# The first norm and the first projection of a decoder trunk: GpSimd taken out, statistics straight from the squares

## The chip, the cores and the metric

The kernel runs on one core of a Trainium2 chip. The metric is device time in microseconds (us), from one launch to its end. The core's engines are TensorE (PE, matrix products; PEld marks its weight loads), VectorE (DVE), ScalarE (ACT), GpSimd (POOL) and SyncE (SP, whose queue issues the transfers). They run side by side, and each works through its own queue in order.

## The reference

Two layers of a decoder trunk, on one sequence of 512 tokens with 1024 features, in float32. Each layer is three sublayers: a feed-forward block (SwiGLU, 2816 hidden), a token mixer, and a second feed-forward block. What the change touches is the start of the first one:

```python
def _rmsnorm(x, g):
    y = x * lax.rsqrt(jnp.mean(x * x, axis=-1, keepdims=True) + EPS)
    return y * g

mod = silu(c) @ ada_w[l] + ada_b[l]          # shift, scale, gate for each sublayer

def _sublayer(x, fn, pre_g, post_g, shift, scale, gate, res_w):
    h = _rmsnorm(x, pre_g) * (1.0 + scale) + shift
    y = _rmsnorm(fn(h), post_g)
    return x + res_w * (1.0 + gate) * y

def _swiglu(h, w13, w2):
    g, u = jnp.split(h @ w13, 2, axis=-1)
    return (silu(g) * u) @ w2
```

## The kernel before, in words

Features lie on the 128 partitions, tokens along the free dimension, so x is eight tiles `xs[f]` of 128x512. Precision comes from splitting both sides of a product: a weight tile is rounded to a high part `wh` (ScalarE, `L250`) and the remainder `wl` (a subtraction, `L251`), h likewise to `hh` and `hl`, and each product is three matmuls: `hh` by `wh`, `hh` by `wl`, `hl` by `wh`.

The first norm and the head of the first feed-forward phase stand in one block in which the program's order is kept on PE, DVE, ACT and SP:

- The conditioning vector c is spread over the partitions by two one-row products (`L1060`) and passed through SiLU into `cb` (`spread`, `L1055` and `L1056`). `spin(n)` issues n products into a bank that nobody reads; `WARM` gives the three counts.
- ACT squares each x tile (`L1079`). Seven additions on POOL and DVE (`add`, `L1072`) bring eight squares down to two tiles, and PE sums those over the partitions into a 128x4 tile `st` (`L1088`): four products of one column per tile, each recorded twice.
- `rsqrt` (`L274` to `L287`) takes the root in nine tiny DVE steps. `rms_bcast` (`L307`) brings it back to the feature layout as `bc`, in PSUM; ACT copies that to `bcs` (`L1112`).
- `ada_block(0, typ, f)` loads 512 KB of the conditioning weights (SP, `L144`) and multiplies them by `cb` with a sum along the row (DVE, `L145`). `ada_fin` turns the sum into one column of scale (two DVE steps, `L155` and `L156`) and one of shift (one step, `L153`).

Then the head: eight steps f. The weights `raw` of step f (512 KB, `L239`, fetched a step ahead) are split, ACT for `wh` and POOL for `wl`. `pre_h` makes h in three steps: DVE forms `tmp` = x times scale column times root (`L340`), ACT adds the shift and rounds to `hh` (`L341`), DVE takes the rest as `hl` (`L342`). The two conditioning products of step f + 1 stand on DVE around `L342`, then its `ada_fin`. PE then runs 24 matmuls of 512 columns into eight banks that stay open over all steps (`mm_start`, `L442`, for the first seven steps, and `mm_k`, `L264` to `L266`, for the last).

The conditioning blocks share two rings of eight buffers with the weights' high and low parts, and raw weights use a ring of four: a load is issued when the tile that had its buffer is done with. SP issues in program order, so a load that waits holds up those behind it. Behind the head, `evac` takes each pair of banks (`L477` to `L479`, `L256`, `L257`), and the remaining 18 pairs follow with PE alone in written order; conditioning loads for later phases are mixed into DVE's work there, using the same four raw buffers.

Of the kernel before, what the change touches and what calls it, by code (L numbers as in the profile page):

```python
# [7 lines left out]
F32 = mybir.dt.float32  # L8
F32R = mybir.dt.float32r
I32 = mybir.dt.int32  # L10
AF = mybir.ActivationFunctionType
ALU = mybir.AluOpType
ADD, SUB, MUL, MAX, MIN = ALU.add, ALU.subtract, ALU.mult, ALU.max, ALU.min

P = 128
D = 1024
T = 512
KT = D // P
# [22 lines left out]
LATE, LATE_Y = 3, 1  # L41
W_0, W_A, W_ST, W_BC, W_UP, W_SQ, W_H = 1.606, 0.51, 1.903, 0.459, 0.81, 2.2, 0.868

WARM = (3, 1, 3)
SPREAD = (1, 3)
NGRP = 7

# [28 lines left out]
def trunk_kernel(ctx: ExitStack, tc: tile.TileContext, a: dict, out: bass.AP):  # L76
    nc = tc.nc
    V, S, PE, G = nc.vector, nc.scalar, nc.tensor, nc.gpsimd

    cst = ctx.enter_context(tc.tile_pool(name="cst", bufs=1))  # L80
# [10 lines left out]
    def t_tmp(w=T):  # L91
        if w == 256:
            return sb.tile([P, w], F32, tag="tmph", bufs=TMPH, name=nm("tmph"))
        return sb.tile([P, w], F32, tag="tmp", bufs=TMP, name=nm("tmp"))
# [16 lines left out]
    def t_st():  # L111
        return ps.tile([P, T], F32, tag="st", bufs=2, name=nm("st"))
# [9 lines left out]
    def vc(name, i=0, w=None):  # L122
        o, n = _OFF[name]
        return vec[:, o + i : o + i + (n - i if w is None else w)]
# [12 lines left out]
    def dcol(ph, typ, f, w=1):  # L137
        o = ph * 24 + typ * 8 + f
        return drv[:, o : o + w]

    def ada_block(ph, typ, f, w=None):
        i = ph * 24 + typ * 8 + f
        w = t_raw() if w is None else w
        nc.sync.dma_start(w, a["ada_w"][i])  # L144
        V.scalar_tensor_tensor(w, w, 0.5, cb, op0=MUL, op1=MUL, accum_out=modc[:, i : i + 1])  # L145

    def ada_fin(ph, typ, f, w):
        i = ph * 24 + typ * 8 + f
        m = modc[:, i : i + w]
        d = dcol(ph, typ, f, w)  # L150
        n = ph * 8 + f
        if typ == 0:
            V.tensor_tensor(d, m, vc("ada_b", i, w), op=ADD)  # L153
            return
        V.tensor_tensor(m, m, vc("ada_b", i, w), op=ADD)  # L155
        V.scalar_tensor_tensor(d, m, 1.0, vc("pre" if typ == 1 else "post", n, w), op0=ADD, op1=MUL)  # L156
        if typ == 2 and ph % 3 != 1:
            V.tensor_scalar(d, d, 0.5, None, op0=MUL)
# [83 lines left out]
    def t_w():  # L242
        return (
            sb.tile([P, 1024], F32R, tag="wh", bufs=8, name=nm("wh")),
            sb.tile([P, 1024], F32R, tag="wl", bufs=8, name=nm("wl")),
        )
# [23 lines left out]
    def rsqrt(src, scale):  # L270

        w = src.shape[1]
        v, y, q, t = t_small(w), t_small(w), t_small(w), t_small(w)
        V.tensor_scalar(v, src, scale * RS_LAM, EPS * RS_LAM, op0=MUL, op1=ADD)  # L274
        V.tensor_scalar(y.bitcast(I32), v.bitcast(I32), -0.5, RS_K, op0=MUL, op1=ADD)
        V.tensor_tensor(q, y, y, op=MUL)
        if w <= 2:
            for i in range(w):
                c = slice(i, i + 1)
                V.tensor_scalar(q[:, c], q[:, c], v[:, c], -RS_M, op0=MUL, op1=ADD)  # L280
        else:
            V.tensor_tensor(q, q, v, op=MUL)
            V.tensor_scalar(q, q, -RS_M, None, op0=ADD)
        V.scalar_tensor_tensor(t, q, RS_B[0], q, op0=ADD, op1=MUL)
        V.scalar_tensor_tensor(t, t, RS_B[1], q, op0=ADD, op1=MUL)
        V.scalar_tensor_tensor(t, t, RS_B[2], q, op0=ADD, op1=MUL)
        V.scalar_tensor_tensor(y, t, RS_B[3], y, op0=ADD, op1=MUL)  # L287
        return y
# [14 lines left out]
    def rms_bcast(y):  # L303
        n = y.shape[1]
        bc = t_st()
        for i in range(n):
            PE.matmul(  # L307
                bc[:, i * P : (i + 1) * P], lhsT=y[:, i : i + 1].to_broadcast([P, P]), rhs=ident, start=True, stop=True
            )
        return bc[:, : n * P]  # L310
# [3 lines left out]
    class SumSq:  # L314
# [7 lines left out]
        def add(self, src):  # L322
            self.n += 1
            if self.n == 1:
                t = t_tmp(T) if self.w == T else sb.tile([P, 256], F32, tag="acc", bufs=3, name=nm("acc"))
                self.acc = t
            else:
                t = t_tmp(self.w)
            S.activation(t, src, AF.Square)  # L329
            if self.n > KT - self.late:  # L330
                self.queue.append((t, lambda: V.tensor_tensor(self.acc, self.acc, t, op=ADD)))
            elif self.n > 1:
                G.tensor_tensor(self.acc, self.acc, t, op=ADD)  # L333
# [5 lines left out]
    def pre_h(ph, f, bc, lo, hi, t):  # L339
        V.scalar_tensor_tensor(t, xs[f][:, lo:hi], dcol(ph, 1, f), bc, op0=MUL, op1=MUL)  # L340
        S.activation(hh[f][:, lo:hi], t, AF.Identity, bias=dcol(ph, 0, f))  # L341
        return lambda: V.scalar_tensor_tensor(  # L342
            hl[f][:, lo:hi], t, dcol(ph, 0, f), hh[f][:, lo:hi].bitcast(F32), op0=ADD, op1=SUB
        )
# [69 lines left out]
    class PairHead(Ready):  # L414
# [21 lines left out]
        def mm_start(self, k):  # L436

            ops = [(b, (2 * p + s) * P) for p in range(self.n) for s, b in enumerate(self.banks[0][p])]
            order = [(0, hh[k]), (0, hl[k]), (1, hh[k])] if k == 0 else [(0, hh[k]), (1, hh[k]), (0, hl[k])]
            for i, (part, h) in enumerate(order):  # L440
                for b, c in ops:
                    PE.matmul(  # L442
                        b, lhsT=self.w[k][part][:, c : c + P], rhs=h, start=(k == 0 and i == 0),
                        stop=(k == KT - 1 and i == 2),
                    )
# [602 lines left out]
    ph = phases[0]  # L1048
    with tc.manual_schedule(engines={nc.tensor.engine, nc.vector.engine, nc.scalar.engine, nc.sync.engine}):
        tag = lambda t: sb.tile([P, 1024], F32, tag=t, bufs=8, name=nm("ad"))  # L1050

        def spread(i):

            c = slice(i * T, (i + 1) * T)
            S.activation(cb[:, c], co[i], AF.Tanh, scale=0.5)  # L1055
            V.scalar_tensor_tensor(cb[:, c], cb[:, c], 1.0, co[i], op0=ADD, op1=MUL)  # L1056

        co = [t_mm(), t_mm()]
        for i in range(2):
            PE.matmul(co[i], lhsT=ones[0:1, :], rhs=crow[0:1, i * T : (i + 1) * T], start=True, stop=True)  # L1060
        warm = t_mm()

        def spin(n):

            for _ in range(n):
                PE.matmul(warm, lhsT=ones, rhs=xs[0], start=True, stop=True)

        sqs = [t_hid() for _ in range(KT)]
        st = t_st()

        def add(e, i, j):
            e.tensor_tensor(sqs[i], sqs[i], sqs[j], op=ADD)  # L1072

        sums = {
            1: [lambda: add(G, 0, 1)], 3: [lambda: add(V, 2, 3), lambda: add(V, 0, 2)],
            5: [lambda: add(V, 4, 5), lambda: add(V, 0, 4)], 7: [lambda: add(V, 6, 7)],
        }
        for f in range(KT):
            S.activation(sqs[f], xs[f], AF.Square)  # L1079
            if f in SPREAD:  # L1080
                spread(SPREAD.index(f))
            for go in sums.get(f, ()):
                go()
        blk = lambda f, typ: ada_block(0, typ, f, tag("wh" if typ else "wl"))
        spin(WARM[0])
        for n, f in enumerate((0, 6)):
            for i in range(4):
                PE.matmul(  # L1088
                    st[:, i : i + 1], lhsT=sqs[f][:, i * P : (i + 1) * P], rhs=ones[:, 0:1],
                    start=(n == 0 and i == 0), stop=(n == 1), skip_group_check=True,  # L1090
                )
        spin(WARM[1])
        blk(0, 1)

        def fin(f):
            ada_fin(0, 1, f, 1)
            ada_fin(0, 0, f, 1)

        y = rsqrt(st[:, :4], 1.0 / D)
        bc = rms_bcast(y)  # L1100
        bcs = t_hid()
        spin(WARM[2])
        blk(0, 0)
        nc.sync.dma_start(vec, a["vec"])
        ph.head.fetch(0)
        fin(0)
        ph.head.alloc(0, T)
        for f in range(KT):
            ph.head.split(f, G)
            low = pre_h(0, f, bc if f == 0 else bcs, 0, T, t_tmp())  # L1110
            if f == 0:
                S.activation(bcs, bc, AF.Copy)  # L1112
                low()
            if f < KT - 1:
                blk(f + 1, 1)
            if f:
                low()
            if f < KT - 1:
                blk(f + 1, 0)
                fin(f + 1)  # L1120
                ph.head.fetch(f + 1)
            ph.head.mm_start(f) if f < NGRP else ph.head.mm_k(f, 0, T, False)
        ph.head.evac(0, T)
# [138 lines left out]
```

## Time and profile before

| | |
|---|---|
| median of 3 runs | 1901.01 us (1900.94 to 1901.99) |
| profiled execution: its own time | 1902.68 us |
| its span | 1901.0 us |
| mean granted TensorE clock | 0.988 |
| busy: PE, DVE, ACT, POOL | 1845.7, 1139.7, 666.7, 186.9 us |
| HBM | 279.15 MB read, 35.65 MB written |

All times of single instructions are us from the span's start. A row of the timeline has start, busy time, engine, line, operation, tile written and tiles read, shape and count; in brackets stand the idle time of the engine before it and what ended it. A row of the chain (the work that ended last, followed back from the end) has start, time, engine and line. A row by stretches has the stretch, its length, the busy time of the engine with its number of records, the granted TensorE clock (1.00 is full), the share of the transfer engines and GB/s. Ends of matmul records are modelled; their starts tell how fast they follow each other.

### The profile page before, as it was taken

What the parts mean: (1) busy time and instruction counts of PE and PEld (TensorE: products, weight loads), DVE (VectorE), ACT (ScalarE), POOL (GpSimd) and SP (SyncE); (2) the same over time, 40 slices, a digit from 0 to 9 for tenths busy, and PEclk for the clock granted to TensorE, in tenths of its full rate; (3) what the DMA queues carried; (4) which work ended last, traced back from release to release, by engine and by line L of the source; (5) the groups of instructions that cost most, each with busy time, mean ns of one, the idle gap of its engine ahead of it and who ended that gap; (6) DMA issues with size and microseconds to landing.
All of it is one profiled execution on the core that took longest, in us unless ns stands there. A gap on an engine that the chain in (4) does not pass through costs nothing.

```text
span 1901.0 us, 24653 instructions
## 1 busy us (share of the span) xinstructions
PE 1845.7 (97%) x9534; PEld 1556.2 (82%) x9534; DVE 1139.7 (60%) x1976; ACT 666.7 (35%) x1008; POOL 186.9 (10%) x175
## 2 busy tenths in 40 slices
PE   8999899999779999999999999999999999999997
PEld 5778688898558988888899888888978998888887
DVE  7976665377994774555347766653586483334434
ACT  3333323235664443323224443332233342222221
POOL 3200000025622000000020000000200200000002
PEclk9999999999889999999999999999999999999999
DMA  8488886232024286565332997773414333333211
GB/s 315 154 300 297 279 288 229 83 128 68 33 73 157 90 282 217 171 191 204 100 131 85 324 316 255 268 250 117 161 58 142 134 103 119 122 100 129 94 45 45
DMA packets 96168, 316.42 MB, mean 166 GB/s; under 512 B 10673, under 2 KB 12849, under 8 KB 96050
## 3 DMA queue, kind: packets, MB, share of 16 engines
q1 hardware_dynamic: 96050, 314.84, 48.9%
q8 instruction: 75, 1.23, 0.3%
q14 instruction: 43, 0.35, 0.1%
HBM read 279.15 MB, written 35.65 MB: 166 GB/s over the span
## 4 chain that ended last, share of the span: by engine, by line
PE 77%; DVE 11%; DMA 6%; ACT 3%; issue 2%; POOL 1%; SPq 0%; DVEq 0%; ACTq 0%; POOLq 0%
PE mm L264 24%; PE mm L266 24%; PE mm L265 24%; DMA raw<-in_w13r_dram 2%; DMA raw<-in_ada_w_dram 2%; DVE wl L251 2%; DMA raw<-in_w13h_dram 1%; ACT wh L250 1%; DMA raw<-in_w_dram 1%; DVE raw L145 1%; DVE ad L145 1%; POOL hid L676 1%; PE st L307 1%; DVE mm L688 1%; DVE wl L848 1%
## 5 line engine op out<-in xcount | busy, mean ns | idle before, releaser
L264 PE MATMUL mm<-hh,wh 128*128 128x512 f32 (+1 forms) x1734 | 644.2, 372 | 4.8 <-ACT hh L341 4.8
L266 PE MATMUL mm<-hl,wh 128*128 128x512 f32 (+1 forms) x1734 | 640.2, 369 | 0.7
L265 PE MATMUL mm<-hh,wl 128*128 128x512 f32 (+1 forms) x1734 | 638.1, 368 | 0.3 <-DVE wl L251 0.3
L250 ACT ACTIVATE wh<-raw 128x1024 fp32r<-128x1024 f32 (+2 forms) x310 | 313.4, 1013 | 520.0 <-PE mm L266 215.1
L251 DVE TENSOR_TENSOR wl<-raw,wh 128x1024 fp32r<-128x1024 f32 (+2 forms) x302 | 351.6, 1167 | 162.0 <-ACT wh L250 152.1
L264 PE MATMUL mm<-hid,wh 128*128 128x256 f32 (+1 forms) x1164 | 386.6, 332 | 8.9 <-ACT hid L256 7.0
L265 PE MATMUL mm<-hid,wl 128*128 128x256 f32 (+1 forms) x1164 | 384.6, 331 | 0.0
L266 PE MATMUL mm<-hid,wh 128*128 128x256 f32 (+1 forms) x1164 | 383.4, 330 | 0.2
L264 PEld LDWEIGHTS mm<-hh,wh 128*128 128x128 f32 x1734 | 327.1, 189 | 63.7 <-ACT hh L341 6.0
L265 PEld LDWEIGHTS mm<-hh,wl 128*128 128x128 f32 x1734 | 326.6, 188 | 61.0 <-issue 2.2
L266 PEld LDWEIGHTS mm<-hl,wh 128*128 128x128 f32 x1734 | 327.0, 189 | 59.1 <-DVE hl L342 2.2
L264 PEld LDWEIGHTS mm<-hid,wh 128*128 128x128 f32 x1164 | 219.9, 189 | 32.9 <-ACT hid L256 8.0
L333 POOL TENSOR_TENSOR acc<-acc,tmph 128x256 f32<-128x256 f32 x112 | 88.2, 793 | 1605.5 <-ACT tmph L329 1601.1
L266 PEld LDWEIGHTS mm<-hid,wh 128*128 128x128 f32 x1164 | 219.7, 189 | 23.8 <-DVE hid L257 1.7
L265 PEld LDWEIGHTS mm<-hid,wl 128*128 128x128 f32 x1164 | 219.8, 189 | 21.3
L145 DVE SCALAR_TENSOR_TENSOR raw<-raw,cb 128x1024 f32<-128x1024 f32 x128 | 155.7, 1221 | 71.7 <-DMA raw<-in_ada_w_dram 71.0
L506 DVE TENSOR_TENSOR y<-y,mm 128x256 f32<-128x256 f32 (+1 forms) x92 | 48.1, 523 | 134.7 <-PE mm L266 134.4
L478 DVE SCALAR_TENSOR_TENSOR tmp<-tmp,mm 128x512 f32<-128x512 f32 x78 | 53.4, 685 | 122.3 <-ACT tmp L477 122.3
L479 DVE SCALAR_TENSOR_TENSOR tmp<-tmp,mm 128x512 f32<-128x512 f32 x78 | 53.5, 686 | 111.1 <-PE mm L266 110.7
L477 ACT ACTIVATE tmp<-mm 128x512 f32<-128x512 f32 x78 | 46.4, 595 | 194.8 <-PE mm L266 194.7
L329 ACT ACTIVATE tmph<-y 128x256 f32<-128x256 f32 x84 | 35.0, 417 | 114.2 <-DVE y L506 112.7
L676 POOL TENSOR_TENSOR hid<-hid,cp 128x507 f32<-128x507 f32 (+10 forms) x44 | 67.3, 1530 | 59.7 <-ACT cp L675 57.2
(204 smaller groups left out, 1275.2 us busy)
## 6 DMA issues: line engine op xcount, KB each, us to landing
raw<-in_w13r_dram SPq DMA_DIRECT2D x150, 512.0 KB, 4.4
raw<-in_ada_w_dram SPq DMA_DIRECT2D x128, 512.0 KB, 4.6
raw<-in_w_dram SPq DMA_DIRECT2D x64, 448.0 KB, 4.2
raw<-in_w_dram SPq DMA_DIRECT2D x32, 512.0 KB, 3.5
kept<-wh SPq DMA_DIRECT2D x32, 384.0 KB, 3.4
kept<-wl SPq DMA_DIRECT2D x32, 384.0 KB, 3.7
wl<-kept SPq DMA_DIRECT2D x32, 384.0 KB, 3.2
wh<-kept SPq DMA_DIRECT2D x32, 384.0 KB, 3.9
```

What stands on the lines that cost most here:

```text
L145: V.scalar_tensor_tensor(w, w, 0.5, cb, op0=MUL, op1=MUL, accum_out=modc[:, i : i + 1])
L250: S.activation(wh[:, :cols], raw[:, :cols], AF.Copy)
L251: eng.tensor_tensor(wl[:, :cols], raw[:, :cols], wh[:, :cols].bitcast(F32), op=SUB)
L264: PE.matmul(o, lhsT=wh, rhs=hi, start=start, stop=False, skip_group_check=shared)
L265: PE.matmul(o, lhsT=wl, rhs=hi, start=False, stop=False, skip_group_check=shared)
L266: PE.matmul(o, lhsT=wh, rhs=lo, start=False, stop=stop, skip_group_check=shared)
L333: G.tensor_tensor(self.acc, self.acc, t, op=ADD)
L477: S.activation(t, g, AF.Tanh, scale=0.5)
L478: V.scalar_tensor_tensor(t, t, 1.0, g, op0=ADD, op1=MUL)
L479: V.scalar_tensor_tensor(t, t, 0.5, u, op0=MUL, op1=MUL)
L506: V.tensor_tensor(self.ys[f][:, lo:hi], self.ys[f][:, lo:hi], o, op=ADD)
L676: G.tensor_tensor(ap[:, s:], ap[:, s:], q[:, s:], op=ADD)
```

## The change

All of it lies in the first block. The seven additions of squares go; PE takes the statistics from all eight squares. x is multiplied by the root first (`norm`, on DVE, in place of the squares). With x normalised, ACT makes the high part of h in one step with the scale and shift columns (`high`), and in a second step the shift minus that high part, into a temporary; DVE then multiplies the normalised x by the scale column and adds the temporary (`low`). The subtraction for `wl` moves from POOL to DVE. `ada_fin` has a form of one step for each single column, with `b1`, the conditioning bias plus one, prepared once. The order of products in `mm_start` is the first step's for all steps (`hh` by `wh`, `hl` by `wh`, `hh` by `wl`). The warm-up counts go from 3, 1, 3 to 1, 1, 1, and the first of them stands ahead of the squares' loop. The transfer of the vector of small parameters is issued after the root's broadcast and ahead of the first shift block; the copy `bcs` stands ahead of the first weights on ACT.

```diff
-WARM = (3, 1, 3)
+WARM = (1, 1, 1)
...
+        if w == 1:
+            if typ == 0:
+                V.tensor_scalar(d, m, vc("ada_b", i, 1), None, op0=ADD)
+            else:
+                V.tensor_scalar(d, m, b1[:, f : f + 1], vc("pre", n, 1), op0=ADD, op1=MUL)
+            return
...
-            order = [(0, hh[k]), (0, hl[k]), (1, hh[k])] if k == 0 else [(0, hh[k]), (1, hh[k]), (0, hl[k])]
+            order = [(0, hh[k]), (0, hl[k]), (1, hh[k])]
...
-        sums = {
-            1: [lambda: add(G, 0, 1)], 3: [lambda: add(V, 2, 3), lambda: add(V, 0, 2)],
-            5: [lambda: add(V, 4, 5), lambda: add(V, 0, 4)], 7: [lambda: add(V, 6, 7)],
-        }
+        spin(WARM[0])
         for f in range(KT):
             S.activation(sqs[f], xs[f], AF.Square)
             if f in SPREAD:
                 spread(SPREAD.index(f))
-            for go in sums.get(f, ()):
-                go()
-        spin(WARM[0])
-        for n, f in enumerate((0, 6)):
             for i in range(4):
                 PE.matmul(
                     st[:, i : i + 1], lhsT=sqs[f][:, i * P : (i + 1) * P], rhs=ones[:, 0:1],
-                    start=(n == 0 and i == 0), stop=(n == 1), skip_group_check=True,
+                    start=(f == 0 and i == 0), stop=(f == KT - 1), skip_group_check=True,
                 )
         spin(WARM[1])
         blk(0, 1)
+        y = rsqrt(st[:, :4], 1.0 / D)
+        bc = rms_bcast(y)
+        spin(WARM[2])
+        nc.sync.dma_start(vec, a["vec"])
+        blk(0, 0)
+        b1 = cst.tile([P, KT], F32, name="b1")
+        V.tensor_scalar(b1, vc("ada_b", KT, KT), 1.0, None, op0=ADD)
...
+        def norm(f, by):
+            V.tensor_tensor(sqs[f], xs[f], by, op=MUL)
+        def high(f):
+            S.activation(hh[f], sqs[f], AF.Identity, scale=dcol(0, 1, f), bias=dcol(0, 0, f))
+            rest[f] = t_tmp()
+            S.activation(rest[f], hh[f].bitcast(F32), AF.Identity, scale=-1.0, bias=dcol(0, 0, f))
+        def low(f):
+            V.scalar_tensor_tensor(hl[f], sqs[f], dcol(0, 1, f), rest.pop(f), op0=MUL, op1=ADD)
         bcs = t_hid()
-        spin(WARM[2])
-        blk(0, 0)
-        nc.sync.dma_start(vec, a["vec"])
+        S.activation(bcs, bc, AF.Copy)
         ph.head.fetch(0)
+        norm(0, bc)
         fin(0)
         ph.head.alloc(0, T)
         for f in range(KT):
-            ph.head.split(f, G)
-            low = pre_h(0, f, bc if f == 0 else bcs, 0, T, t_tmp())
-            if f == 0:
-                S.activation(bcs, bc, AF.Copy)
-                low()
+            wh, wl = t_w()
+            raw = ph.head.raw.pop(f)
+            ph.head.w[f] = wh, wl
+            S.activation(wh, raw, AF.Copy)
+            high(f)
+            V.tensor_tensor(wl, raw, wh.bitcast(F32), op=SUB)
+            low(f)
             if f < KT - 1:
+                norm(f + 1, bcs)
                 blk(f + 1, 1)
-            if f:
-                low()
-            if f < KT - 1:
                 blk(f + 1, 0)
                 fin(f + 1)
                 ph.head.fetch(f + 1)
```

More of the change, by code (lines that the diff above doesn't have):

```diff
@@ L1069, in trunk_kernel @@
         st = t_st()
-        def add(e, i, j):
-            e.tensor_tensor(sqs[i], sqs[i], sqs[j], op=ADD)
-        sums = {
-            1: [lambda: add(G, 0, 1)], 3: [lambda: add(V, 2, 3), lambda: add(V, 0, 2)],
-            5: [lambda: add(V, 4, 5), lambda: add(V, 0, 4)], 7: [lambda: add(V, 6, 7)],
-        }
+        blk = lambda f, typ: ada_block(0, typ, f, tag("wh" if typ else "wl"))
+        spin(WARM[0])
         for f in range(KT):
@@ L1081, in trunk_kernel @@
                 spread(SPREAD.index(f))
-            for go in sums.get(f, ()):
-                go()
-        blk = lambda f, typ: ada_block(0, typ, f, tag("wh" if typ else "wl"))
-        spin(WARM[0])
-        for n, f in enumerate((0, 6)):
             for i in range(4):
@@ L1097, in fin @@
             ada_fin(0, 0, f, 1)
-        y = rsqrt(st[:, :4], 1.0 / D)
-        bc = rms_bcast(y)
+        def norm(f, by):
+            V.tensor_tensor(sqs[f], xs[f], by, op=MUL)
+        rest = {}
+        def high(f):
[4 more added lines that the diff above has]
+            V.scalar_tensor_tensor(hl[f], sqs[f], dcol(0, 1, f), rest.pop(f), op0=MUL, op1=ADD)
         bcs = t_hid()
-        spin(WARM[2])
-        blk(0, 0)
-        nc.sync.dma_start(vec, a["vec"])
+        S.activation(bcs, bc, AF.Copy)
         ph.head.fetch(0)
+        norm(0, bc)
         fin(0)
```

## The prediction

> **What bounds the kernel now.** I read the page first: its chain of the work that ended last gives TensorE (PE) three quarters of the span.
>
> ```profile
> PE 77%; DVE 11%; DMA 6%; ACT 3%; issue 2%; POOL 1%; SPq 0%; DVEq 0%; ACTq 0%; POOLq 0%
> ```
>
> The change touches only the first 73 us, so I read the timeline of all engines from 0 to 73 us, then the chain of the same stretch, then PE and its granted clock in stretches of 3.41 us. The timeline shows the way to the head's first matmul (start us, us busy, engine, line, [idle before]).
>
> ```profile
> 6.08 5.20 PE L1066 MATMUL mm<-x,ones 128*128 128x512 f32 x6
> 8.65 2.24 ACT L1079 ACTIVATE hid<-x 128x512 f32<-128x512 f32 x4
> 9.39 3.42 DVE L1072 TENSOR_TENSOR hid<-hid,hid 128x512 f32<-128x512 f32 x5
> 12.26 1.95 PE L1088 MATMUL st<-ones,hid 128*128 128x1 f32 x16 [0.98 <-DVE hid L1072]
> 14.24 0.16 DVE L274 TENSOR_SCALAR sm<-st 128x4 f32<-128x4 f32 x1 [0.29 <-PE st L1088]
> 15.77 2.34 POOL L251 TENSOR_TENSOR wl<-raw,wh 128x1024 fp32r<-128x1024 f32 x1 [9.26 <-ACT wh L250]
> 15.83 2.29 DVE L287 SCALAR_TENSOR_TENSOR sm<-sm,sm 128x4 f32<-128x4 f32 x1
> 18.27 2.05 PE L307 MATMUL st<-ident,sm 128*128 128x128 f32 x8 [2.33 <-DVE sm L287]
> 20.11 3.23 PE L1066 MATMUL mm<-x,ones 128*128 128x512 f32 x6
> 21.14 0.72 ACT L341 ACTIVATE hh<-tmp,drv 128x512 fp32r<-128x512 f32 x1 [5.45 <-DVE tmp L340]
> 21.76 0.58 ACT L1112 ACTIVATE hid<-st 128x512 f32<-128x512 f32 x1
> 22.77 1.96 PE L442 MATMUL mm<-hh,wh 128*128 128x512 f32 x6
> ```
>
> Squares end at 10.89, their sums on VectorE (DVE) at 12.2, the 16 statistics records at 14.2. The last tiny DVE step, 128x4, takes 2.29 us because it runs exactly as long as the GpSimd (POOL) subtraction beside it; its neighbours take 0.16. The head starts at 22.77, behind the last of three warm-up products.
>
> In the head I read one of the even steps, first its chain, then its timeline, then rows from its ends.
>
> ```profile
> 29.46 0.67 DVE hl L342
> 30.12 1.14 DVE ad L145 x2
> 31.27 2.33 DVE modc L155
> ```
>
> ```profile
> 28.98 1.05 ACT L250 ACTIVATE wh<-raw 128x1024 fp32r<-128x1024 f32 x1
> 30.11 3.46 POOL L251 TENSOR_TENSOR wl<-raw,wh 128x1024 fp32r<-128x1024 f32 x1 [4.01 <-ACT wh L250]
> 31.09 1.56 PE L442 MATMUL mm<-hh,wl 128*128 128x512 f32 x6
> 32.95 1.56 PE L442 MATMUL mm<-hl,wh 128*128 128x512 f32 x6
> 35.38 1.67 PE L442 MATMUL mm<-hh,wh 128*128 128x512 f32 x6 [0.40 <-ACT hh L341]
> 66.61 0.50 PE L264 MATMUL mm<-hh,wh 128*128 128x512 f32 x1 [0.39 <-ACT hh L341]
> 67.54 1.22 DVE L251 TENSOR_TENSOR wl<-raw,wh 128x1024 fp32r<-128x1024 f32 x1 [0.20 <-ACT wh L250]
> 72.57 0.39 PE L264 MATMUL mm<-hh,wh 128*128 128x512 f32 x1
> ```
>
> A 128x1 addition holds DVE for 2.33 us until POOL's subtraction ends: DVE sets the step. Step 2 starts at 35.38 and step 7 at 66.61, so a step is 31.23 / 5 = 6.25 us, while its 24 matmuls need 24 x (32.95 - 31.09) / 8 = 5.6.
>
> **The change part by part.** *The head's steps.* POOL's subtraction goes to DVE (1.22, the 67.54 row, which is DVE's own). A step of DVE then is 1.22 for the weights, a wait for ScalarE, 0.67 for the low part, 0.68 for the normalisation (a fifth of the 3.42 us row), two conditioning products of 1.15, and two tiny steps instead of three, some 0.3. The wait: ScalarE needs 2 x 0.72 + 0.05 for the two steps on h while DVE works 1.22 on the weights, so 0.27. Sum 5.4, below the 5.6 of PE: PE becomes the bound. ScalarE has 1.05 + 2 x 0.72 = 2.5 per step, hidden. Before, the head took 72.57 - 22.77 = 49.8 us from its first matmul to the next phase's; eight steps of 5.6 are 44.8. Gain 5.0 at full clock. If DVE's step came to 5.7 this would lose 0.1 x 6.
>
> *The sums on DVE and POOL* (3.42 us) go; their place is taken by 64 statistics records in place of 16, on PE, in its order behind one warm-up product instead of three. That product is two of the six records of 5.20 us, so it ends at 6.08 + 2 x 0.855 = 7.79, and from there the squares are ready as PE reaches them (the last at 10.89). What does a record cost? At 12.26 sixteen take 1.95, 0.112 each. But the clock decides, so here are PE's busy time and granted clock on its own grid (us, length, PE busy (records), clock, DMA).
>
> ```profile
> 4.02:7.43 3.41, 3.41 (x5) 1.00 0.91 280
> 7.43:10.85 3.42, 3.42 (x5) 1.00 1.04 399
> 10.85:14.26 3.41, 2.43 (x18) 1.00 1.03 418
> 14.26:17.68 3.42, 1.68 (x2) 0.50 1.03 420
> 17.68:21.09 3.41, 2.82 (x10) 0.50 1.02 418
> 21.09:24.50 3.41, 3.41 (x12) 1.00 1.03 417
> 485.31:488.72 3.41, 2.63 (x10) 0.50 0.02 5
> 505.79:509.20 3.41, 3.41 (x10) 0.50 0.36 111
> ```
>
> The first two rows say 1.00 only because the trace has no clock event yet: six passes of 512 columns take 5.20 us from 6.08 and 3.23 from 20.11, where the clock rises at 21.09, so PE is at half clock until 10.85. Five records filled 7.43 to 10.85 and the clock was full behind them; 2.82 us of 3.41 was enough at 17.68, 2.63 at 485.31 was not. But 3.41 busy us at 4.02, mostly products of one row, did not raise it, and 2.43 at 10.85, mostly one-column statistics, lost it again. Statistics therefore count little. After the change one product of 512 columns stands alone in front of them: I take the clock to be half through all 64 records.
>
> At half clock the weights set their pace. The rows are weight loads at 18 us (128 columns) and, at 509 us, across the clock's edge at 509.20, for a two-column product.
>
> ```profile
> 18.62 0.33 PEld L307 LDWEIGHTS st<-ident,sm 128*128 128x128 f32 x1
> 18.83 0.33 PEld L307 LDWEIGHTS st<-ident,sm 128*128 128x128 f32 x1
> 509.06 0.26 PEld L708 LDWEIGHTS st<-grp,tmp 128*128 128x128 f32 x1
> 509.24 0.19 PEld L708 LDWEIGHTS st<-grp,tmp 128*128 128x128 f32 x1
> ```
>
> At half clock one follows the other after 0.213 us. At the edge 0.14 us were spent at half clock: with 0.213 per load 0.34 of it is left, 0.04 us at full clock, and the next would follow at 509.24, as it does; with 0.112 it would have come at 509.17. So the bounds of a record are 0.112 and 0.213; I take 0.213. Then the records take 63 x 0.213 + 0.4 = 13.8 and end at 21.65, not 14.2.
>
> Here a page of the Trainium skill speaks otherwise. "TensorE: Matmul & The Clock Gate", section "LDWEIGHTS (loading the stationary operand)", gives a load as its columns over 1.2 GHz with no word of the clock, an estimate of 0.107 us: by it the sum would be the first rival's. The rows at 18 and 509 us disagree.
>
> *From the statistics to the head.* The nine steps of the root lose POOL's stall: 15.83 - 14.24 + 0.3 = 1.9 to the first broadcast, 23.55. The broadcast takes 2.05 + 0.05 at half clock: 25.65. Then ScalarE's queue has the copy of it (0.6), the first weights' high part (1.05; in the kernel before this ran long ahead, and now it stands behind the copy) and h (0.72): head at 28.1. DVE's normalisation of 0.68 and its two tiny steps run beside the copy and the weights; uncovered they would cost 1.0. The warm-up product after the broadcast, 0.85 to 1.7 us, ends by 27. Start: 28.1 - 22.77 = +5.3.
>
> *The head's clock.* The stretch 24.50 to 27.92 holds some 0.8 of broadcast and 1.7 of warm-up, below the 2.63 that failed, so the head begins at half clock until the next edge, 31.33: 3.2 us at half rate, 1.6 lost. The grid may stand otherwise in another execution; ends 0 (no cold stretch) and 3.4 (two stretches). I take 1.6, which this grid gives.
>
> *Queues.* The vector's DMA moves ahead of one 512 KB load on SP's queue: that load, not awaited before 23.5, comes some 0.6 later, free. The conditioning product of the first shift block runs after the root, which ends at 23.4 instead of 18.1, so SP, whose buffers go round after four steps, waits with the fifth step's loads until some 24.6 and with its weights until DVE is done with the first ones, 28.5; they are used from 28.1 + 3 x 5.4 = 44 us on, which hides it. Without that cover each us would cost one. Adding one to the vector (0.16) hides under the broadcast.
>
> **Sum.** +5.3 - 5.0 + 1.6 = +1.9 us on the profiled execution (span 1901.0, own time 1902.68): 1904.6. The median of the three runs, 1901.01, lies 1.7 lower; to it 1902.9.
>
> **Carried to the end?** Behind the head, PE runs on to 227.8 and then waits for the loads' loop.
>
> ```profile
> 212.81 0.66 issue
> 213.46 0.68 DVE tmp L478
> 225.24 5.45 DMA raw<-in_ada_w_dram
> ```
>
> ```profile
> 234.27 0.80 PE L264 MATMUL mm<-hid,wh 128*128 128x512 f32 x1 [6.46 <-ACT hid L256]
> ```
>
> The loop itself waited for PE's result 0.66 us at 212.81, so a later PE moves the loop's last part as well, whose transfers (5.45 us at 225.24) follow it: the shift is carried. If it were not, up to 6.46 us of wait could swallow it.
>
> **The rivals.** *1. The statistics run at 0.112*, because single columns keep the array busy enough for the full clock, or because loads do not follow the clock. Then they end near 15.2 and the head starts 6.4 earlier, at 21.7, with 17.68 to 21.09 filled by broadcast and warm-up and so at full clock: 21.7 - 22.77 - 5.0 = -6.1, 1894.9. If the clock rises only at 10.85, 14 records pass at 0.213 and 50 at 0.112, 1.4 us later: 1896.3. For it: the row at 12.26; against it: the rows of the clock at 4.02 and 10.85 and the loads at 509. By "TensorE: Matmul & The Clock Gate", Part 1, some 3.4 us of sustained activity release the clock, which PE, busy from 2.40, would have behind it by 7.43; this trace, at half clock until 10.85, does not bear that out for one-row products. *2. DVE still bounds the step* (slower): if the wait for ScalarE, in order behind the weights' high part, stretches DVE's step to today's 6.25, the second step comes at 28.1 + 5.5 and the eighth at 33.6 + 37.5 = 71.1, 4.5 after today's 66.61, and it saves 0.4 in itself: +4.1, 1905.1. It decides from about 6.2 us per step. For it: DVE has 0.2 us of slack in my sum, and ScalarE's queue is new in its way; against it: the 2.33 are POOL's alone. *3. The wait at 227.8 swallows the loss*: DVE would end the head's last low part at 28.5 + 7 x 5.4 + 0.7 = 67, where it does now (the row of 67.54 follows on it), so the load loop starts unmoved, and if it alone sets 234.27 nothing changes: 1901.0. Against: the 0.66.
>
> **How the numbers follow.** Forecast 0.46, rival 1 0.22, rival 2 0.12, rival 3 0.20. A change of 0.2%, 3.8 us, is about what a measurement of this kernel can tell from none. Faster: most of rival 1, 0.20. Slower: two thirds of rival 2 and, with two cold stretches (+3.7) and a little noise, a sixth of the forecast: 0.16. The rest, 0.64, within. The range runs from rival 1, 1895, to rival 2 with a little beyond, 1905.5; the forecast alone spans 1901 to 1905.
>
> **What would show it.** The 64 statistics records at 0.213 each, ending near 21.6; the head's first matmul near 28; PE without waits between steps, 5.6 us each; no 128x1 step of DVE over 0.2 us; the next phase's first matmul at 74.5 (now 72.57). Statistics that end before 17 make the prediction wrong, as do steps over 6 us, or a wait at 228 that changes by more than the shift.

## The result, and the profile after

The changed kernel takes 1912.96 us (median of 4 runs, 1910.61 to 1913.43) beside 1900.97 us for the kernel before (4 runs, 1899.91 to 1901.99): a ratio of 1.0061, with a 95% interval of 1.0043 to 1.0078. It is 12.0 us slower; the forecast was 1.9 us slower, and the time lies above the end of the range. The profiled execution has an own time of 1913.43 us and a span of 1911.7 us, 10.7 more than the span before. The mean clock is 0.989 (0.988 before), so the clock as a whole is not the cause.

The share of PE in the chain of the work that ended last goes from 77% to 79%, and DVE's from 11% to 9%:

```profile
PE 79%; DVE 9%; DMA 6%; ACT 3%; issue 2%; POOL 1%; SPq 0%; DVEq 0%; ACTq 0%; POOLq 0%
```

The timeline of the changed kernel up to the head's first matmuls, and the same view of its steps 5 and 6, counted from 0 (start us, us busy, engine, line, [idle before]; what were lines 264 to 266 and 442 are now 271 to 273 and 449):

```profile
8.02 13.65 PE L1085 MATMUL st<-ones,hid 128*128 128x1 f32 x64
21.71 0.16 DVE L281 TENSOR_SCALAR sm<-st 128x4 f32<-128x4 f32 x1 [8.30 <-PE st L1085]
23.61 2.05 PE L314 MATMUL st<-ident,sm 128*128 128x128 f32 x8
25.69 0.60 ACT L1118 ACTIVATE hid<-st 128x512 f32<-128x512 f32 x1 [12.79 <-PE st L314]
26.19 1.05 ACT L1127 ACTIVATE wh<-raw 128x1024 fp32r<-128x1024 f32 x1
26.32 0.69 DVE L1104 TENSOR_TENSOR hid<-x,st 128x512 f32<-128x512 f32 x1 [1.64 <-ACT hid L1118]
27.35 0.81 ACT L1110 ACTIVATE hh<-hid,drv 128x512 fp32r<-128x512 f32 x1
28.22 1.67 PE L449 MATMUL mm<-hh,wh 128*128 128x512 f32 x6 [1.02 <-ACT hh L1110]
56.32 1.56 PE L449 MATMUL mm<-hh,wh 128*128 128x512 f32 x6
60.48 0.27 DVE L157 TENSOR_SCALAR drv<-modc,b,vec 128x1 f32<-128x1 f32 x1
61.93 1.57 PE L449 MATMUL mm<-hh,wh 128*128 128x512 f32 x6
```

This much is as forecast. The 64 statistics records follow each other every 13.65 / 64 = 0.213 us and end at 21.67 (21.65 forecast). The head starts at 28.22 (28.1 forecast). Its steps 5 and 6 start 61.93 - 56.32 = 5.61 us apart, PE has no waits between them, and DVE's 128x1 steps take 0.27 at most where 2.33 stood before. DVE's own step is just as long: its subtractions for `wl` start at 55.19 and 60.78, 5.59 apart. The last step starts at 67.55, 0.94 later than the 66.61 of before. Up to here the change costs one microsecond. The rest follows.

The last step of the head in the timeline, and PE's busy time and granted clock by stretches around it (us, length, PE busy (records), clock, DMA share, GB/s):

```profile
67.22 1.04 ACT L257 ACTIVATE wh<-raw 128x1024 fp32r<-128x1024 f32 x1
67.55 0.39 PE L271 MATMUL mm<-hh,wh 128*128 128x512 f32 x1
68.17 0.71 ACT L1112 ACTIVATE tmp<-hh,drv 128x512 f32<-128x512 f32 x1
68.29 1.22 DVE L258 TENSOR_TENSOR wl<-raw,wh 128x1024 fp32r<-128x1024 f32 x1 [0.70 <-ACT wh L257]
69.44 0.74 DVE L1115 SCALAR_TENSOR_TENSOR hl<-hid,drv,tmp 128x512 fp32r<-128x512 f32 x1
70.23 0.50 PE L273 MATMUL mm<-hl,wh 128*128 128x512 f32 x1 [2.07 <-DVE hl L1115]
77.01 0.40 PE L271 MATMUL mm<-hh,wh 128*128 128x512 f32 x1
```

```profile
64.44:67.86 3.42, 3.42 (x17) 1.00 0.12 47
67.86:71.27 3.41, 1.34 (x6) 1.00 0.62 180
71.27:74.67 3.40, 3.40 (x10) 0.50 0.38 128
```

On ACT the high part of the next chunk's weights (67.22) stands ahead of the second step on h (68.17), and on DVE the remainder of those weights (68.29) stands ahead of the low part (69.44). PE waits 2.07 us for the low part, is busy for 1.34 of 3.41 us, and runs the following stretch at half clock. The loss of the clock needs the wait and the place of the stretch both: in `r1_b1_modc` below the same wait falls across two stretches and costs no clock. The last step takes 77.01 - 67.55 = 9.46 us; before it took 72.57 - 66.61 = 5.96. The shift, the start of a product after less that of the same product before, grows from +0.94 to +4.44 us.

Two further waits, the load-loop wait and a wait much later, in PE's timeline:

```profile
95.57 0.50 PE L271 MATMUL mm<-hh,wh 128*128 128x512 f32 x1 [1.75 <-ACT wh L257]
96.83 0.50 PE L272 MATMUL mm<-hh,wl 128*128 128x512 f32 x1 [0.76 <-DVE wl L258]
239.68 0.80 PE L271 MATMUL mm<-hid,wh 128*128 128x512 f32 x1 [5.51 <-ACT hid L263]
716.89 0.50 PE L271 MATMUL mm<-hid,wh 128*128 128x512 f32 x1 [1.19 <-ACT hid L263]
```

The first two lift the shift to +6.4 us (at 111 us); the third is a little shorter than before (5.51 beside 6.46) and leaves +5.41 (239.68 - 234.27). From there the shift grows to +10.82 at the start of the last long stretch of 384 products of h's parts with weights. 1.4 us of this come at 717 us, in the wait of 1.19 shown and one of 0.21 a microsecond later; PE waits at neither place in the kernel before. The rest comes steadily, 0.4 us by 692 and behind 717 some 0.35 us in every 110 us, and no wait does it. The first and the last product of that stretch, before and then after:

```profile
1753.60 0.39 PE L264 MATMUL mm<-hh,wh 128*128 128x512 f32 x1
1841.70 0.39 PE L266 MATMUL mm<-hl,wh 128*128 128x512 f32 x1
```

```profile
1764.42 0.39 PE L271 MATMUL mm<-hh,wh 128*128 128x512 f32 x1
1852.94 0.39 PE L273 MATMUL mm<-hl,wh 128*128 128x512 f32 x1
```

The 383 intervals take 88.10 us before and 88.52 after: 230.0 and 231.1 ns for the same product, at full clock, with nothing waited for. Over all products behind 239 us the slower pace makes 4.4 us: 3.8 from those of h's parts with 512 columns and 0.6 from those with 256. About half of the loss is therefore far outside the block that was changed.

### The profile page after: what moved, and what is told of

Its sections match the earlier page's. It is cut to its first block, busy times and chain, and to the rows that moved or that the text cites. A ratio compares the mean times of both kernels' runs of the same rounds, so it can differ in the third digit from the quotient of the medians.

```text
span 1911.7 us, 24725 instructions
## 1 busy us (share of the span) xinstructions
PE 1857.6 (97%) x9574; PEld 1566.8 (82%) x9574; DVE 1127.1 (59%) x1972; ACT 674.0 (35%) x1016; POOL 159.9 (8%) x166
## 4 chain that ended last, share of the span: by engine, by line
PE 79%; DVE 9%; DMA 6%; ACT 3%; issue 2%; POOL 1%; SPq 0%; DVEq 0%; ACTq 0%; POOLq 0%
PE mm L273 25%; PE mm L271 24%; PE mm L272 24%; DMA raw<-in_w13r_dram 2%; DVE wl L258 1%; DMA raw<-in_ada_w_dram 1%; DMA raw<-in_w_dram 1%; ACT wh L257 1%; DVE raw L145 1%; DMA raw<-in_w13h_dram 1%; POOL hid L683 1%; PE st L1085 1%; PE st L314 1%; PE mm L449 1%; DVE mm L695 1%
## 5 line engine op out<-in xcount | busy, mean ns | idle before, releaser
L257 ACT ACTIVATE wh<-raw 128x1024 fp32r<-128x1024 f32 (+2 forms) x302 | 305.1, 1013 | 533.5 <-PE mm L273 210.2
L263 ACT ACTIVATE hid<-tmp 128x512 fp32r<-128x512 f32 x87 | 54.1, 622 | 57.0 <-DVE tmp L486 46.6
```

Of the source, the lines that this page charges most:

```text
L257: S.activation(wh[:, :cols], raw[:, :cols], AF.Copy)
L263: S.activation(hi, src, AF.Copy)
```

## The experiments

The means below are spacings of consecutive products after 75 us, in ns, worked out from the starts in each trace. "h parts" are the products of `hh` and `hl` with the weights, 512 columns (4050 of 128x512) and 256 columns (1152). Spacings that hold a wait or half clock are left out; how strictly moves the means of `hid` with 512 columns by up to 0.5 ns, and no reading below rests on so little.

```
kernel                      h parts 512   h parts 256   hid 512   hid 256
before                           230.07         118.7    230.64    117.77
after                            231.15         119.3    230.69    117.77
e1_pad32    before + 32 B        231.15         119.3    230.71    117.77
r1_b1_modc  after, unmoved       230.07         118.5    230.66    117.77
r2_pad128   before + 128 B       231.11         117.8    230.66    117.76
e2_b1_64    after, 64 B          232.86         116.1    230.62    117.79
p1_wl64     before, 64 B gap     233.2          118.9    226.48    119.92
```

**The changed kernel again, and the places of the tiles.** The only thing in the change that reaches the whole program is the new tile `b1`, 32 bytes per partition. In the compiled programs it moves every tile allocated after it by 32 bytes, while `hh`, `hl` and x stay:

```
byte offset in a partition   hh0     hl0     raw     hid     wh      wl
before                       40896   57280   75072   91456   124224  157184
after                        40896   57280   75104   91488   124256  157216
```

Two theories stood for the slower pace. A: the places of the tiles set it. B: it is a matter of the chip or the hour, not of the kernel. A third, that the drift comes with the late head, which shifts transfers against products, is taken up with `r1_b1_modc`. First the changed kernel once more, and the kernel before with nothing but an unused 32-byte tile:

> The changed kernel again, on the chip and in the rounds of the three kernels beside it. Theory A (addresses: the 32 bytes of b1 move every working tile behind it off a multiple of 64 bytes, and each product from then on is some 0.3% slower): 1912 to 1913, and products at full clock in the later phases that follow each other 0.3% later than before's. Theory B (the slower pace of the products is a matter of the chip or the hour, not of the kernel): nearer to before on this chip, some 1907.

Measured for `e0_after`: 1909.49 us (6 runs, 1905.65 to 1911.82), ratio 1.0036 (1.0023 to 1.0048), so +7.4 beside the +12.0 of the first measurement. In its profiled execution, its fastest at 1905.65, the wait of the load loop is 1.20 us:

```profile
234.07 0.50 PE L271 MATMUL mm<-hid,wh 128*128 128x512 f32 x1 [1.20 <-ACT hid L263]
```

The head is as late as in the first trace, but here some 7 us come back: the wait is 5.3 us shorter than that of the kernel before, and PE keeps the full clock behind it, where the first twelve products behind the wait of before follow each other after 0.43 us or more. The length of this wait differs between executions of one kernel, and the two traces show where that begins. In the chain, the same load of weights is issued at the same time, first in the first trace of the changed kernel, then here:

```profile
88.45 5.99 DMA raw<-in_w13r_dram
88.45 4.69 DMA raw<-in_w13r_dram
```

Loads wait for buffers in order, so the loop of loads is 1.3 us ahead from there on, and it gains further: the load on which the load-loop wait depends is issued at 224.75 instead of 230.71. Why a transfer takes longer in one execution is not shown. The time, 1909.49, lies between the theories' figures and does not decide between them; the pace does. It is there again, 231.16 ns, and the drift with it. The unused tile in the kernel before:

```diff
+        pad = cst.tile([P, KT], F32, name="pad")
+        V.memset(pad, 0.0)
```

> The kernel before with one unused tile of 32 bytes per partition at the place where the change puts b1, written once (0.1 us). Nothing else differs. Theory A: slower by 5 to 6 us, 1906 to 1907, with a shift against before that grows evenly from the first phase to the last. Theory B: as before, 1901 within 1 us.

Measured: 1904.59 us (11 runs), ratio 1.0014 (1.0005 to 1.0022). The last stretch in its timeline:

```profile
1755.07 0.39 PE L264 MATMUL mm<-hh,wh 128*128 128x512 f32 x1
1843.58 0.39 PE L266 MATMUL mm<-hl,wh 128*128 128x512 f32 x1
```

88.51 us: the pace of the changed kernel, with none of its other edits. That is theory A; its figure for the time, 1906 to 1907, was too high. In its trace the shift against before is -2.3 us at 234 and +1.6 at 1787, a drift of 3.9. That it is ahead early has another reason, in the timeline of its start:

```profile
15.27 0.16 DVE L287 SCALAR_TENSOR_TENSOR sm<-sm,sm 128x4 f32<-128x4 f32 x1
15.56 3.29 POOL L251 TENSOR_TENSOR wl<-raw,wh 128x1024 fp32r<-128x1024 f32 x1 [9.08 <-ACT wh L250]
```

The statistics came 0.6 us earlier here, and the last tiny step of the root ended before POOL's subtraction began, so the stall of 2.29 us that the profile of before shows does not occur. The two are a few tenths of a microsecond apart. The stall is missing in the traces of `r2_pad128` and `p1_wl64` too, and only one trace of the kernel before is kept, so how often it occurs there is not shown.

**A rule for the places?** First guess: the tiles have to keep their distance to a multiple of 64 bytes. `b1` was made 64 bytes wide in the changed kernel:

```diff
-        b1 = cst.tile([P, KT], F32, name="b1")
+        b1 = cst.tile([P, 2 * KT], F32, name="b1")[:, 0:KT]
```

> The changed kernel with b1 allocated twice as wide, 64 bytes, of which it uses the first 32; all queues hold the same instructions in the same order. Theory A: faster than the changed kernel by 5 to 6 us, 1907, and no growing shift against before after 250 us. Theory B: as the changed kernel, 1912 to 1913.

Measured: 1915.71 us (5 runs), ratio 1.0065 (1.0052 to 1.0077): not faster, and the products are slower still. Two of its long stretches in PE's timeline, first and last product of each:

```profile
866.84 0.39 PE L271 MATMUL mm<-hh,wh 128*128 128x512 f32 x1
955.36 0.39 PE L273 MATMUL mm<-hl,wh 128*128 128x512 f32 x1
1763.63 0.40 PE L271 MATMUL mm<-hh,wh 128*128 128x512 f32 x1
1853.27 0.40 PE L273 MATMUL mm<-hl,wh 128*128 128x512 f32 x1
```

Within one kernel 384 products take 88.52 us in one phase and 89.64 in another (231.1 and 234.0 ns). The guess of 64 bytes fell. That the places set the pace did not: this kernel and the changed one hold the same instructions and differ by 32 bytes of a tile's width, and the pace goes from 231.15 to 232.86. The second guess was that the offset between the moving operand and the weights counts modulo 128 bytes, with zero best; a gap of 64 bytes between the rings of `wh` and `wl`, in the kernel before, was to make products faster:

```diff
+        gap = sb.tile([P, 16], F32, tag="gap", bufs=1, name="gap")
+        V.memset(gap, 0.0)
```

> The kernel before with one unused tile of 64 bytes per partition between the ring of the weights' high parts and that of their low parts (written once, 0.1 us). In the runs so far the 512-column products of hh and hl with the weights follow each other after 230.07 ns (before), 231.15 (weights moved by 32 bytes against hh and hl) and 232.86 (by 64), while those of hid, which moves with the weights, stay at 230.6 to 230.7. Theory P (a product's pace goes by the distance of its moving operand from its weights, modulo 128 bytes, 0 the best and 64 the worst; before, the high parts stand at 0 and the low parts at 64): with both at 0 some 227 to 228 ns, 5202 such products, 10 to 15 us faster, 1887 to 1892. Rival (it is no matter of 128 bytes, or of the weights against h, but of other tiles that moved along): no such gain, within 3 us of before or slower.

Measured: 1910.19 us (5 runs), ratio 1.0047 (1.0034 to 1.0059).

```profile
1760.72 0.40 PE L264 MATMUL mm<-hh,wh 128*128 128x512 f32 x1
1850.08 0.39 PE L266 MATMUL mm<-hl,wh 128*128 128x512 f32 x1
```

89.36 us here, 233.3 ns. The products of h's parts got slower, those of `hid` with 512 columns faster (226.48), those with 256 columns slower (119.92). By the counts in the profile's groups (4050, 1500 and 1992) that is 4050 x 3.1 - 1500 x 4.2 + 1992 x 2.15 = some +10.5 us; +9.5 was measured. So the second guess fell too, but the size of the loss follows from the paces. The table also shows that the distance between the operands matters: `hid` moves along with the weights in every other run and keeps its pace there; only here, where the low weights move against it, does it change. Last, 128 bytes in the place of the 32:

```diff
+        pad = cst.tile([P, 4 * KT], F32, name="pad")
+        V.memset(pad, 0.0)
```

> The kernel before with one empty tile of 128 bytes per partition (written once by VectorE, read by nobody) in the place where the changed kernel has its 32 bytes. Theory A (the pace goes by addresses modulo 128 bytes): 230.07 ns per product of h's parts with the weights, 117.77 and 230.6 for the others, and the time of the kernel before, 1900 to 1902. Theory B (the pace goes by the distance between moving operand and weights over a longer period, or by which end of the memory they lie in): another pace, 231 to 233 ns, and 5 to 15 us more. Theory C (any tile in this place costs, wherever the others land, because of the writing itself): about the 1904.6 of the 32-byte tile, pace 231.15.

Measured: 1902.5 us (10 runs), ratio 1.0012 (1.0001 to 1.0023).

```profile
1751.92 0.39 PE L264 MATMUL mm<-hh,wh 128*128 128x512 f32 x1
1840.43 0.40 PE L266 MATMUL mm<-hl,wh 128*128 128x512 f32 x1
```

88.51 us: not the pace of before, so a period of 128 bytes is excluded (theory A of that run). The pace alone would also fit its theory C, that the writing of any tile in this place costs; that falls by `e2_b1_64`, which writes the same as the changed kernel and is slower, and by the next run, which writes it too and has the pace of before. The total is near that of before because, in the trace, the 256-column products run at 117.8 instead of 118.7 (1.0 us), the start, like that of `e1_pad32`, has no stall in the root (1.4) and the load-loop wait is shorter (4.8 us, 1.7 less). Which rule the pace follows stays open.

**The tile alone, taken out of the changed kernel.** `b1` in eight columns of an existing tile that get their own values only much later; no tile moves, all else is the changed kernel:

```diff
-        b1 = cst.tile([P, KT], F32, name="b1")
+        b1 = modc[:, 136:144]
```

> The changed kernel with one edit: the eight values of bias plus one stand in eight unused columns of the tile of conditioning columns, so that no later tile moves; queues, order and statistics stay as in the changed kernel. Theory 1 (the 32 bytes set the pace of the products of h's parts with the weights): spacing of these products back from 231.15 to 230.07 ns, no steady drift behind the head, and 4 to 6 us below the changed kernel's 1909.5 to 1913, so 1904 to 1909; step 7 of the head still waits 2.1 us for the low part and takes 9.5 us. Theory 2 (the drift comes with the shift of the head against the loads, not with addresses): the pace stays at 231.15 and the time at 1910 to 1913.

Measured: 1907.1 us (10 runs, 1903.78 to 1908.65), ratio 1.0027 (1.0018 to 1.0037).

```profile
70.27 0.50 PE L273 MATMUL mm<-hl,wh 128*128 128x512 f32 x1 [2.09 <-DVE hl L1115]
1757.50 0.39 PE L271 MATMUL mm<-hh,wh 128*128 128x512 f32 x1
1845.60 0.39 PE L273 MATMUL mm<-hl,wh 128*128 128x512 f32 x1
```

The wait in the head's last step is as long as in the changed kernel, but the last stretch takes 88.10 us again, and the shift goes from +4.3 at 238 to +3.9 at 1554. The drift is gone with the move of the tiles; theory 2 of this run, by which the pace had to stay with the late head, fell. So did B: `r2_pad128` ran beside this kernel on the same chip, at the slower pace. The time is 5.9 us below the first measurement of the changed kernel and 2.4 below the second; the interval of the second (1.0023 to 1.0048) overlaps this one, so it is the pace that tells the two apart, not the time.

The last step of the head was expected at 9.5 us and took 75.44 - 67.50 = 7.94. PE by stretches that end where this trace's clock can change (counted back in steps of 3.41 us from 96.05, where it falls):

```profile
68.74:72.16 3.42, 1.89 (x8) 1.00 0.84 252
72.16:75.57 3.41, 3.41 (x16) 1.00 0.26 80
```

The wait lies across 68.74, so neither stretch is as empty as the 1.34 us of the changed kernel, and the clock stays. It is lost at 96.05 instead, behind a stretch with 1.45 us of products and the waits of 1.67 and 0.77 that stand there in this kernel: at 98 us the shift is +6.9, beside +7.1 in the changed kernel. Where the stretches lie is a matter of the execution (in `e0_after`, the changed kernel again, one ends at 70.32 instead of 71.27), so it is luck whether this wait costs clock.

**The order in the last step.** The next chunk's weights are held behind the head's last ACT and DVE instruction; all else is the changed kernel, `b1` included:

```diff
+        ends = [
+            next(i for i in reversed(nc.cur_bb.bb.instructions) if i.engine == e.engine) for e in (S, V)
+        ]
...
+                if n == 0:
+                    for i in ends:
+                        es.enter_context(tc.issue_after(i))
                 ph.rest()
```

> The changed kernel with the splits of the next weights held behind the head's last two steps on ScalarE and VectorE (rest(7) and low(7)); nothing else is changed, b1 has its 32 bytes. If the 2.07 us wait of PE for hl(7) and the half clock behind it come from that order alone, both go: 3 to 4 us faster than the changed kernel, 1909. If the wait comes from the chain normalise, high, rest, low itself, it stays, and the time with it.

Measured: 1907.84 us (11 runs), ratio 1.0032 (1.0023 to 1.0041).

```profile
67.97 1.04 ACT L257 ACTIVATE wh<-raw 128x1024 fp32r<-128x1024 f32 x1
68.10 0.75 DVE L1115 SCALAR_TENSOR_TENSOR hl<-hid,drv,tmp 128x512 fp32r<-128x512 f32 x1 [0.52 <-ACT tmp L1112]
68.90 0.49 PE L273 MATMUL mm<-hl,wh 128*128 128x512 f32 x1 [0.72 <-DVE hl L1115]
```

The low part comes 1.34 us earlier, PE waits 0.72 instead of 2.07 and keeps the full clock, and the two waits of the changed kernel at 95 and 97 are gone with it: the shift at 111 us is +2.3. Against the 1909.49 of the changed kernel beside it this is only 1.7 us, with intervals that overlap; 3 to 4 were expected. At 111 us its trace is 2.8 us ahead of that of `e0_after` (+5.1) and 4.1 ahead of the first trace of the changed kernel (+6.4); the load-loop wait then takes part of it.

Both at once, the order held and no tile moved:

> The changed kernel with the order at the head's end mended as in the run before, and with b1 kept in columns of an existing tile that are written only much later, so that no tile moves. If placement is worth 5202 products of 1.08 ns, 5.6 us less than with the order alone: 1902, and products of hh at 230.07 ns. If placement matters only in the profile's pace and not in the time: as the order alone, 1908.

Measured: 1903.74 us (11 runs), ratio 1.0014 (1.0005 to 1.0023), 3.1 us above the 1900.68 of before in the same comparison. This is the change as the prediction priced it, and the prediction had +1.9, which lies within the interval (+1.0 to +4.4). The products of h's parts follow each other after 230.1 ns, as expected; the time was to fall by 5.6 against the order alone and fell by 4.1, or by 2.7 when each is taken against the kernel before beside it. Its head starts at 28.07 and its shift at 111 us is +1.0, the forecast without the term for the clock (+0.3) and a little for the last step; its load-loop wait is 3.36 us long in the profiled execution, which is the shortest of the eleven (1901.08).

**Which part of the change is worth keeping.** As the last, but with the statistics of before (sums on POOL and DVE, 16 records, three warm-up products); the head's new steps stay:

> As the run beside it (order mended, no tile moved), with the statistics of the kernel before: squares added to two tiles by GpSimd and VectorE, 16 records in place of 64, three warm-up products ahead of them and one behind. If the 64 records at half clock cost the start what the prediction put (statistics end at 21.7 instead of 14.2), the head's first matmul comes at 21 to 22.5 instead of 28.2 and the time falls by 5 to 7 us, to 1895 to 1897. If the start is covered by the load loop that follows, the time stays near 1902.

Measured: 1896.2 us (11 runs), ratio 0.9971 (0.9962 to 0.998), 7.5 us below the last.

```profile
12.14 2.53 PE L1095 MATMUL st<-ones,hid 128*128 128x1 f32 x16 [1.38 <-DVE hid L1080]
14.71 0.16 DVE L281 TENSOR_SCALAR sm<-st 128x4 f32<-128x4 f32 x1 [0.88 <-PE st L1095]
21.21 1.66 PE L449 MATMUL mm<-hh,wh 128*128 128x512 f32 x6 [0.90 <-ACT hh L1120]
```

The root starts at 14.71 instead of 21.71 and the head at 21.21 instead of 28.07: 6.9 us by the trace. The statistics from eight squares are the part of the change that costs. What pays is the rest of it: the head's last step starts at 60.52, 6.09 before that of the kernel before, 1.56 of this from the earlier start and 4.53 from the seven steps. One step more, the first weights' high part ahead of the copy of the broadcast on ACT:

```diff
+        first = t_w()
+        S.activation(first[0], ph.head.raw[0], AF.Copy)
         S.activation(bcs, bc, AF.Copy)
```

> As the statistics' run beside it, with the first weights' high part ahead of the copy of the broadcast on ScalarE. If that order costs the start its 1.05 us as put, the head begins 1 us earlier and the time falls by about 1; if DVE's normalisation and tiny steps or the warm-up product behind the broadcast end last there, by less than 0.5.

Measured: 1895.31 us (9 runs), ratio 0.9971 (0.9961 to 0.998), the same.

```profile
14.26 0.16 DVE L281 TENSOR_SCALAR sm<-st 128x4 f32<-128x4 f32 x1 [0.68 <-PE st L1095]
18.87 0.69 DVE L1114 TENSOR_TENSOR hid<-x,st 128x512 f32<-128x512 f32 x1 [1.63 <-ACT hid L1131]
20.77 1.67 PE L449 MATMUL mm<-hh,wh 128*128 128x512 f32 x6 [0.85 <-ACT hh L1120]
```

From the root to the head it takes 20.77 - 14.26 = 6.51 us, and 21.21 - 14.71 = 6.50 without it. The weights are out of the way, but DVE's normalisation waits for the copy and takes just as long behind it. These two kernels are faster than both the kernel before and the changed one.

## Why the prediction was wrong

Its own steps, in its order:

- **The head's steps, -5.0: right for seven of the eight.** 5.61 us beside 5.6, PE without waits, DVE's stall gone. Rival 2 (DVE still bounds the step, at 6.25) did not happen, but it was closer than the sum said: DVE's step is 5.59, not 5.4, because ScalarE's first step on h takes 0.82 instead of 0.72 and DVE waits 0.51 for it instead of 0.27. Nothing is left of the 0.2 of slack.
- **The last step: the first step that failed.** The prediction made "eight steps of 5.6" out of a sum for the inner steps. The last step ends against the next chunk's weights, and the new form has one more step on ACT between the high and the low part of h, so that the low part on DVE can fall behind them. It was 9.46 us long, some 3.5 longer than before, and two waits at 95 and 97 us followed, 2.0 more at 111 us. In the trace of `e3_order` the order alone takes away all of this but 0.6 in the step itself. Of the 3.5, 2.0 are the wait and what hangs on it; the rest is the half clock, which `r1_b1_modc` met elsewhere.
- **The statistics, 0.213 each: right.** They ended at 21.67 (21.65). That it is so near is in part luck: they started at 8.02 instead of 7.79 and took 13.65 instead of 13.8. Rival 1, at 0.112, fell, and so does the figure of the Trainium skill that spoke for it: "TensorE: Matmul & The Clock Gate", section "LDWEIGHTS (loading the stationary operand)", gives columns over 1.2 GHz, an estimate of 0.107 us for 128 columns, and all 64 records here took twice that at half clock.
- **From the statistics to the head, +5.3: the sum right (+5.45), a piece of it wrong.** The prediction ran DVE's normalisation beside ACT's copy; it waited for the copy (26.32, behind 25.69 + 0.60). The weights that were to cost 1.05 ran beside it instead, so the sum did not change. `e6_wh_first` shows that the weights were not the bound.
- **The head's clock, +1.6: came to 0, and the sum was wrong.** The head's first six matmuls took 1.67 us, which is full clock. The prediction put 0.8 of broadcast and 1.7 of warm-up into the stretch 24.50 to 27.92; but by its own times the broadcast lasts until 25.65, 1.15 us of that stretch, which makes 2.85, above the 2.82 that had been enough. In `r1_b1_modc` the stretch lay almost there, 24.37 to 27.78, held 3.02 and raised the clock. The clock was lost at 71.27 instead, with the wait of the last step.
- **"Adding one to the vector (0.16) hides under the broadcast": the other step that failed.** The instruction is indeed hidden; the tile that it writes is not. It moves the weights by 32 bytes against `hh` and `hl`, and behind 239 us 3552 products of 1.08 ns more and 1152 of some 0.6 make 4.4 us. With the 1.4 of the two waits at 717 us this is what the trace gains from there to the last long stretch's end. What those two waits come from is open; `e0_after` gains the same 1.4 there and `e4_place_order`, with no tile moved, 2.1, so it is not the pace. The prediction priced instructions and waits and took the pace of a product as given.
- **Carried to the end: mostly.** The wait of the load loop was 5.51 beside 6.46, so 1.0 was swallowed in the profiled execution; but in `e0_after` it was 1.20, and some 7 came back. So rival 3 is in part a matter of the execution, not of the kernel: the loads behind the wait took different times in two executions of one kernel. Why they did is open, and with it the difference between +12.0 and +7.4 us in the two measurements of the changed kernel.

In one line, by the profiled execution: +0.9 forecast part, +3.5 last step, +2.0 two waits behind it, -1.0 load loop, +4.4 pace, +1.4 two waits at 717, -0.5 in the tail, that is +10.7, as the span. By the comparisons, the changed kernel stands at 1.0061 and 1.0036; undoing the placement alone leaves 1.0027, the order alone 1.0032, both 1.0014, and these with the old statistics 0.9971. The intervals of either alone overlap that of 1.0036, so each of the two causes is shown by the traces rather than by the time; both together lie clear of the first measurement and at the edge of the second.

## What to carry to other kernels

Where PE runs thousands of equal products, a new tile is an edit to all of them if it is allocated ahead of their operands: put a small new value into a corner of an existing tile, or compare the spacing of the products before and after. When a loop body is rewritten, cost its last turn by itself, with the order of what comes next on each queue. And price single-column matrix products by the clock that will be granted while they run: seven additions on two engines with nothing else to do were cheaper than 48 more records at half clock.

## What the runs showed of the hardware

- The pace of a 512-column product at full clock depends on where its operands lie: 226.5 to 234.0 ns over five placements that differ by 32 to 128 bytes, in steps that differ by operand and by width. The rule is open.
- A stretch of 3.41 us with 1.34 us of products (the changed kernel, 67.86) or 1.45 (`r1_b1_modc`, 92.64) lost the full clock for the next; one with 1.89 us (`r1_b1_modc`, 68.74) kept it. So where a wait lies against these stretches decides whether it costs clock.
- 64 single-column products back to back never raised the clock: all ran at 0.213 us, 13.65 us long, against 0.112 each for the sixteen of the kernel before at 12.26.
- One load of 512 KB, issued at 88.45 us in two executions of the changed kernel, took 5.99 us in one and 4.69 in the other.
